# A hybrid mixer and MLP layer on one core: masked score copies on all partitions at once, a values pass with the width outermost, a last tile in two halves

## The chip, the cores and the metric

The kernel runs on one core of one Trainium2 chip. The metric is the device time of one execution in microseconds (us); lower is better. The kernel before takes 1099.75 us (median of 3 runs, 1098.73 to 1100.7).

The engines are called by what they do here: TensorE (PE) multiplies matrices, and PEld is its loading of the stationary operand; VectorE (DVE) and ScalarE (ACT) do elementwise work; GpSimd (POOL) does a little of it; SyncE (SP) issues most transfers. Each engine works through its instructions in program order.

## The reference

One decoder layer, 1024 tokens of width 1024, all in float32:

```python
h = rms_norm(x, norm_mix_g)
u = h @ w_in                                  # pool 256 | q 768 | f 768 | i 768 | g 768
y_pool = pool_mixer(u_pool, pool_w, pool_scale)
y_hgrn = hgrn2_mixer(q_raw, f_raw, i_raw, g_raw, lower_bounds, hgrn_norm_g)
x = x + concatenate([y_pool, y_hgrn]) @ w_out
h2 = rms_norm(x, norm_mlp_g)
x = x + square(relu(h2 @ w_up)) @ w_down
return rms_norm(x, final_norm_g)
```

The recurrent mixer has 6 heads of 128 channels. With `f = lb + (1-lb) sigmoid(z)`, `k = (1-lb) sigmoid(-z)`, `q = silu(q_raw)` and `v = i_raw`, a head's output at position t is the sum over s <= t of `(q_t * k_s * product of f from s+1 to t) . v_s`, then normed per head and gated by `silu(g_raw)`.

## The kernel before, in words

**Numbers in pairs.** Each matmul operand is split into a high and a low part: ScalarE copies it with rounding (L116, or L246 for x), VectorE subtracts (L117, L247). A product is three matmuls (`mm3`, L122 to L124): high by high, high by low, low by high.

**The start (L211 to L396).** TensorE runs 14 warm-up matmuls (L216). SyncE loads the transposed x in two halves of 512 tokens, each in four pieces of 512 KB (`load_xt`, tiles `xt`), and between the first ones the values weights of the first two heads in two pieces of 512 KB (`raw_v`). Then come four row tiles of x (`load_rows`, tiles `xn`, in the two one-buffer tags T and Kn), the weights of q (`raw_q`) and f (`raw_f`) of head 0, the second half of x, and four more row tiles. Behind these stand small constants and, in a two-buffer ring, the weights that follow. The row tiles only serve for the norm's scale: ScalarE squares and sums them (L255), VectorE and GpSimd make the reciprocal root (L257, L259), and TensorE transposes it (`pt_rms`) into `rms_row`.

For each half, TensorE first makes the values (`dense_V`, four token tiles of 256 columns, in the `dense` banks), with the token tile outside and the 8 width tiles of 128 inside; then q (`gated`) and f (`forget`). ScalarE copies the values out of their banks with the norm's scale (`scaled_V`, L298). A bank can be reused when that is done.

**The heads (L398 to L626).** TensorE's order is written out by hand. A head's recurrence is the generator `hgrn`, which yields how many steps of other work (the next head's projections, `beside`; a step is mostly three matmuls of 512 columns) TensorE does before it goes on (`LAGS`). A chunk of 128 tokens has two half chunks of 64. The scores within a half chunk are made by levels: the diagonal and the neighbours (`sc_near`), then pairs at distances 2, 4, 8, 16 and 32 (`sc`), each after the elementwise products of q and k with the decays (`deepen`, L519, L520) and ScalarE's gathering of the keys and queries (`kq`, L438, L439). The scores of a level lie in a PSUM bank of a ring of two. VectorE picks the valid ones with predicated copies into `scores`, a tile of 8 chunks by 128 x 128. Its two half chunks lie on 64 partitions each and at different columns, so the copies are made by stretches of 32 or 64 partitions: 4 with `dmask` (L424) and 4 with `lmask` (L428) for the nearest, then 4 per level (L452). The scores between half chunks (L462) are copied by ScalarE (L466, L467). Then the keys are transposed, the states chained, and the output is a product of `scores` with the values.

The forget gate's K is `sigmoid(-z)` from ScalarE (L328), multiplied by `om = 1-lb` on VectorE (L329); F is scaled on GpSimd (L330). `om` comes from a short chain at the start (L374 to L384) that uses both VectorE and ScalarE. F, Q and K have two buffers each.

**The MLP and the end (L628 to L1099).** Up and down projections run in blocks that share products; TensorE has no gap there. The final sums into x (L662) are followed by the norm. For the last two products VectorE, ScalarE and GpSimd work in written order: of each of the eight token tiles the left 512 columns come last. A tile's steps are add (VectorE, L662), squares and sum (ScalarE, L991), the mean (VectorE, L1004), the reciprocal root (GpSimd, L1006), then the two products with it (VectorE L1011, ScalarE L1012) and two stores. The products of a tile are written behind the next tile's add and squares.

Of the kernel before, what the change touches and what calls it, by code (L numbers as in the profile page):

```python
# [17 lines left out]
P = 128  # L18
# [42 lines left out]
def kernel(  # L61
# [110 lines left out]
    with ExitStack() as pa:  # L172
        cmix = pa.enter_context(tc.tile_pool(name="cmix", bufs=1))
        dmask = cmix.tile([P, 32], U8, name="dmask")
# [44 lines left out]
        def load_xt(h, b, tag, bufs=2):  # L219
            t = ha.tile([P, 2, HALF], F32, tag=tag, name=f"xt_{h}_{b}", bufs=bufs)  # L220
            nc.sync.dma_start(t, x_t_v[:, 2 * b:2 * b + 2, h * HALF:(h + 1) * HALF])
            return t

        def load_rows(i):
            t = ha.tile([P, D], F32, tag=("T", "Kn")[i % 2], name=f"xn_{i}", bufs=1)
            nc.sync.dma_start(t, x[0, i * P:(i + 1) * P, :])
# [8 lines left out]
        pool.memset(scores, 0.0)  # L235

# [5 lines left out]
        def split_xt(t, h, b):  # L242
            for e in range(2):
                j = 2 * b + e
                hi, lo = hT[h][0][:, j, :], hT[h][1][:, j, :]
                act.activation(hi, t[:, e, :], AF.Copy, scale=g1[:, j:j + 1])  # L246
                dve.scalar_tensor_tensor(  # L247
                    out=lo, in0=t[:, e, :], scalar=g1[:, j:j + 1], in1=hi.bitcast(F32), op0=ALU.mult, op1=ALU.subtract
                )
# [24 lines left out]

        def dense_V(pair, ws, i):

            if i == 0:
                for hd in (2 * pair, 2 * pair + 1):
                    vts[hd] = ha.tile([P, NT, P], F32, tag="V", name=f"V_{hd}", bufs=3)
# [44 lines left out]
        def forget(f, k, w, h, hd):  # L324
# [4 lines left out]
            dve.tensor_scalar(k, k, om[:, hd:hd + 1], None, op0=ALU.mult)  # L329
            pool.tensor_scalar(f, f, om[:, hd:hd + 1], lb[:, hd:hd + 1], op0=ALU.mult, op1=ALU.add)  # L330

        def head_tiles(hd):
            return [ha.tile([P, S], F32, tag=tag, name=f"{tag}_{hd}") for tag in "QFK"]
# [10 lines left out]
        xts, xns, w0 = {}, [], []  # L344
        for b, tag in enumerate("QQKK"):
            xts[0, b] = load_xt(0, b, tag)
            split_xt(xts[0, b], 0, b)
            if b < 2:
                c0 = V0
                w0.append(load_w(w_in_v[:, 4 * b:4 * b + 4, c0:c0 + 256], [4, 256], f"v0_{b}"))  # L350
        xns = [load_rows(i) for i in range(4)]
        wq = q_weights(0)
        wf = f_weights(0)
        for b, tag in enumerate("FFGS"):
            xts[1, b] = load_xt(1, b, tag, 2 if tag == "F" else 1)
            split_xt(xts[1, b], 1, b)
# [15 lines left out]
        act.copy(dmask, mraw[:, 2 * len(LEVELS), :])  # L372
# [31 lines left out]
        def hgrn(hd, q, f, k, vt):  # L404
# [17 lines left out]
            for g in range(4):  # L422
                pr = slice(g * 32, (g + 1) * 32)
                dve.copy_predicated(  # L424
                    sc[pr, :, pr], dmask[pr, None, :].to_broadcast([32, NT, 32]),
                    ps[pr, :256].rearrange("p (c x) -> p c x", x=32),
                )
                dve.copy_predicated(  # L428
                    strided(sc[pr], 1 + g * 32, [(HALF - 1, 2), (P, NT // 2), (2, 16)]),
                    lmask[pr, 0:2, :, g % 2 * 16:g % 2 * 16 + 16],  # L430
                    ps[pr, 256:384].rearrange("p (a c x) -> p a c x", a=2, x=16),
                )
            for li, m in enumerate(LEVELS[1:], 1):
# [15 lines left out]
                for g in range(2):  # L449
                    pr = slice(g * 64, (g + 1) * 64)  # L450
# [703 lines left out]
```

## Time and profile before

| | |
|---|---|
| median of 3 runs | 1099.75 us |
| the profiled execution | 1100.17 us |
| its span | 1098.4 us |
| mean granted clock of TensorE | 0.997 of full speed |
| busy: TensorE, VectorE, ScalarE, GpSimd | 1079.2, 791.8, 422.0, 81.9 us |
| bytes moved | 137.55 MB, 125 GB/s |

The span runs from the first instruction to the end of the last; the execution's own time is 1.8 us longer. A line of the profile names the source line, the engine, the operation, what is written from what (output<-inputs, buffer numbers left out), and the sizes (partitions x elements). In a timeline the first two numbers are the start and the duration in us; a bracket gives how long the engine was idle before it and what ended that. In a list by form, "busy, mean ns | idle before" follow the count. In a list of waits, an arrow points from the engine and line that waited to what it waited for. Matmuls overlap, and their ends are modelled.

### The profile page before, as it was taken

What the parts mean: (1) busy time and instruction counts of PE and PEld (TensorE: products, weight loads), DVE (VectorE), ACT (ScalarE), POOL (GpSimd) and SP (SyncE); (2) the same over time, 40 slices, a digit from 0 to 9 for tenths busy, and PEclk for the clock granted to TensorE, in tenths of its full rate; (3) what the DMA queues carried; (4) which work ended last, traced back from release to release, by engine and by line L of the source; (5) the groups of instructions that cost most, each with busy time, mean ns of one, the idle gap of its engine ahead of it and who ended that gap; (6) DMA issues with size and microseconds to landing.
All of it is one profiled execution on the core that took longest, in us unless ns stands there. A gap on an engine that the chain in (4) does not pass through costs nothing.

```text
span 1098.4 us, 14269 instructions
## 1 busy us (share of the span) xinstructions
PE 1079.2 (98%) x5728; PEld 894.1 (81%) x5728; DVE 791.8 (72%) x1068; ACT 422.0 (38%) x647; POOL 81.9 (7%) x124
## 2 busy tenths in 40 slices
PE   8989999999999999999999999999999999999996
PEld 6868797879887788888888888888888888888885
DVE  4498847784679861599768657855988968677774
ACT  6745343333343431444332233224244333333343
POOL 1001010101010101110011001101100000000001
PEclk9999999999999999999999999999999999999998
DMA  9521102110210162314445335427993354344104
GB/s 313 152 57 31 36 20 58 39 40 21 58 39 20 42 227 87 115 49 154 149 180 189 112 137 191 144 94 267 368 359 148 115 192 153 115 182 162 39 1 153
DMA packets 71362, 137.55 MB, mean 125 GB/s; under 512 B 4864, under 2 KB 44928, under 8 KB 67712
## 3 DMA queue, kind: packets, MB, share of 16 engines
q1 hardware_dynamic: 60656, 100.98, 27.1%
q0 software_dynamic: 9344, 33.56, 7.8%
q10 hardware_dynamic: 1296, 2.10, 0.5%
q8 instruction: 45, 0.74, 0.3%
q14 instruction: 21, 0.17, 0.1%
HBM read 98.87 MB, written 37.75 MB: 124 GB/s over the span
## 4 chain that ended last, share of the span: by engine, by line
PE 85%; DVE 8%; issue 2%; DMA 2%; ACT 2%; POOL 1%; SPq 0%; ACTq 0%; POOLq 0%
PE ps_dx L123 5%; PE ps_ua L124 5%; PE ps_ua L122 5%; PE ps_dx L124 5%; PE ps_dx L122 5%; PE ps_ua L123 5%; PE ps_o L122 3%; PE ps_dy L123 3%; PE ps_uc L124 3%; PE ps_uc L122 3%; PE ps_dy L124 3%; PE ps_dy L122 3%; PE ps_uc L123 3%; PE ps_o L123 3%; PE ps_o L124 3%
## 5 line engine op out<-in xcount | busy, mean ns | idle before, releaser
L116 ACT CAST wdop<-raw_wd 128x2048 fp32r<-128x2048 f32 x28 | 53.6, 1914 | 156.1 <-PE ps_dy L124 49.3
L122 PE MATMUL ps_ua<-h2op,whi_wu 128*128 128x512 f32 x256 | 99.7, 389 | 0.0
L124 PE MATMUL ps_ua<-h2op,wlo_wu 128*128 128x512 f32 x256 | 99.6, 389 | 0.0
L123 PE MATMUL ps_ua<-h2op,whi_wu 128*128 128x512 f32 x256 | 99.6, 389 | 0.0
L122 PE MATMUL ps_dx<-wdop,hop 128*128 128x512 f32 x256 | 99.6, 389 | 0.0
L123 PE MATMUL ps_dx<-wdop,hop 128*128 128x512 f32 x256 | 99.6, 389 | 0.0
L124 PE MATMUL ps_dx<-wdop,hop 128*128 128x512 f32 x256 | 99.6, 389 | 0.0
L117 DVE TENSOR_TENSOR wdop<-raw_wd,wdop 128x2048 fp32r<-128x2048 f32 x28 | 64.1, 2290 | 29.1 <-ACT wdop L116 29.1
L117 DVE TENSOR_TENSOR hop<-hraw,hop 128x2048 fp32r<-128x2048 f32 x28 | 64.0, 2284 | 2.9 <-ACT hop L116 2.9
L116 ACT CAST hop<-hraw 128x2048 fp32r<-128x2048 f32 x28 | 53.4, 1910 | 31.0 <-DMA hraw<-hid 19.5
L117 DVE TENSOR_TENSOR wlo_wu<-raw_wu,whi_wu 128x1024 fp32r<-128x1024 f32 x23 | 28.0, 1222 | 47.8 <-ACT whi_wu L116 47.8
L116 ACT CAST whi_wu<-wsum 128x1024 fp32r<-128x1024 f32 x22 | 23.2, 1054 | 93.9 <-DVE wsum L659 47.5
L662 DVE TENSOR_TENSOR x<-ps_dx,x 128x512 f32<-128x512 f32 x64 | 43.9, 688 | 20.3 <-PE ps_dx L124 20.3
L122 PE MATMUL ps_v<-whi_v,hT_hi 128*128 128x256 f32 x192 | 54.5, 285 | 2.5 <-ACT whi_v L116 1.9
L122 PEld LDWEIGHTS ps_dx<-wdop,hop 128*128 128x128 f32 x256 | 48.1, 188 | 10.0
L123 PEld LDWEIGHTS ps_ua<-h2op,whi_wu 128*128 128x128 f32 x256 | 48.1, 188 | 10.0
L124 PEld LDWEIGHTS ps_ua<-h2op,wlo_wu 128*128 128x128 f32 x256 | 48.1, 188 | 10.0
L123 PEld LDWEIGHTS ps_dx<-wdop,hop 128*128 128x128 f32 x256 | 48.1, 188 | 9.9
L124 PEld LDWEIGHTS ps_dx<-wdop,hop 128*128 128x128 f32 x256 | 48.1, 188 | 9.9
L122 PEld LDWEIGHTS ps_ua<-h2op,whi_wu 128*128 128x128 f32 x256 | 48.1, 188 | 9.8
L123 PE MATMUL ps_v<-wlo_v,hT_hi 128*128 128x256 f32 x192 | 54.3, 284 | 0.8 <-DVE wlo_v L117 0.8
L124 PE MATMUL ps_v<-whi_v,hT_lo 128*128 128x256 f32 x192 | 54.1, 284 | 0.0
(242 smaller groups left out, 2780.2 us busy)
## 6 DMA issues: line engine op xcount, KB each, us to landing
hid<-hid POOLq DMA_DIRECT2D x56, 512.0 KB, 3.2
hraw<-hid SPq DMA_DIRECT2D x28, 1024.0 KB, 5.2
raw_wu<-in_w_up_dram SPq DMA_DIRECT2D x32, 512.0 KB, 3.8
raw_wd<-in_w_down_dram SPq DMA_DIRECT2D x16, 1024.0 KB, 7.1
xt<-in_x_t_dram SPq DMA_DIRECT2D x8, 512.0 KB, 8.0
xn<-in_x_dram SPq DMA_DIRECT2D x8, 512.0 KB, 7.1
x<-x_mid SPq DMA_DIRECT2D x8, 512.0 KB, 5.8
raw_v<-in_w_in_dram SPq DMA_DIRECT2D x6, 512.0 KB, 3.8
```

The source lines that it names most:

```text
L116: act.copy(hi, src)
L117: dve.tensor_tensor(out=lo, in0=src, in1=hi.bitcast(F32), op=ALU.subtract)
L122: pe.matmul(ps, lh, rh, start=start, stop=False, skip_group_check=goes_on)
L123: pe.matmul(ps, lh, rl, start=False, stop=False, skip_group_check=goes_on)
L124: pe.matmul(ps, ll, rh, start=False, stop=stop, skip_group_check=goes_on)
L662: dve.tensor_tensor(out=out_, in0=a, in1=b, op=ALU.add)
```

## The change

There are five edits.

1. **Scores within a half chunk.** A new tile `within` holds, for all 128 partitions, 8 chunks of 64 columns: the scores of a partition's own half chunk. The predicated copies now work on all 128 partitions: two pairs for the nearest (even and odd blocks of 32 by a mask of two parts) and one per level, 9 a head instead of 28. When all levels are in, ScalarE copies `within` into the two diagonal blocks of `scores` with two copies of 64 partitions.
2. **K's scaling** by `om` moves from VectorE to ScalarE (`act.mul`).
3. **The start.** x and the first values weights come in pieces of 256 KB (one width tile of x, two width tiles of weights), split piece by piece. The first values pass has the width outermost: per width tile three matmuls for each of four token tiles, which share two banks of the `misc` ring of three. The row tiles lie in the six buffers that the mixer's outputs use later, and the q weights are asked for after two of them.
4. **Buffers.** F has one buffer, Q and K keep two; the second half of x borrows other tags.
5. **The last tile.** In the last product the last token tile is made in two halves of 256 columns, each with its own add, squares and sum.

The core of the diff:

```diff
+        within = ha.tile([P, NT, P // 2], F32, name="within", tag="within", bufs=1)
...
+        def load_xt(h, tags):
+            for j in range(KT):
+                if j % 2 == 0:
+                    t = ha.tile([P, 2, HALF], F32, tag=tags[j // 2][0], name=f"xt_{h}_{j // 2}", bufs=tags[j // 2][1])
+                nc.sync.dma_start(t[:, j % 2, :], x_t_v[:, j, h * HALF:(h + 1) * HALF])
+                split_xt(t[:, j % 2, :], h, j)
+                yield j
+        def first_V(h, ws):
+            banks = [misc_ps(f"ps_v0_{h}_{i}") for i in range(2)]
+            for j in range(KT):
+                w = ws[j // 4]
+                for i in range(4):
+                    c = i * P
+                    mm3(
+                        banks[i // 2][:, i % 2 * 256:(i % 2 + 1) * 256],
+                        (hT[h][0][:, j, c:c + P], hT[h][1][:, j, c:c + P]),
+                        (w[0][:, j % 4, :], w[1][:, j % 4, :]),
+                        j == 0 and i % 2 == 0, j == KT - 1, i % 2 == 1,
+                    )
+            return banks
...
-            t = ha.tile([P, D], F32, tag=("T", "Kn")[i % 2], name=f"xn_{i}", bufs=1)
+            t = mixp.tile([P, D], F32, tag="mix", name=f"xn_{i}")
...
-            dve.tensor_scalar(k, k, om[:, hd:hd + 1], None, op0=ALU.mult)
+            act.mul(k, k, om[:, hd:hd + 1])
...
-        xns = [load_rows(i) for i in range(4)]
+        xns = [load_rows(i) for i in range(2)]
         wq = q_weights(0)
+        xns += [load_rows(i) for i in range(2, 4)]
         wf = f_weights(0)
...
-            vps = [finish(dense_V(0, w0, i)) for i in (4 * h, 4 * h + 2)]
+            vps = first_V(h, w0)
...
-            for g in range(4):
-                pr = slice(g * 32, (g + 1) * 32)
+            for e in range(2):
                 dve.copy_predicated(
-                    sc[pr, :, pr], dmask[pr, None, :].to_broadcast([32, NT, 32]),
-                    ps[pr, :256].rearrange("p (c x) -> p c x", x=32),
+                    within[:, :, e * 32:(e + 1) * 32], dmask[:, e, None, :].to_broadcast([P, NT, 32]),
+                    ps[:, :256].rearrange("p (c x) -> p c x", x=32),
                 )
...
-                for g in range(2):
-                    pr = slice(g * 64, (g + 1) * 64)
-                    for a in range(2):
-                        dve.copy_predicated(
-                            strided(sc[pr], g * 64 + (a * HALF or m), [(P, NT // 2), (2 * m, 32 // m), (1, m)]),
-                            lmask[pr, 2 * li + a, :, :].rearrange("p j (n m) -> p j n m", m=m),
-                            ps[pr, a * P:(a + 1) * P].rearrange("p (j n m) -> p j n m", j=NT // 2, m=m),
-                        )
+                dve.copy_predicated(
+                    strided(within, m, [(S // 4 - m, 2), (P // 2, NT // 2), (2 * m, 32 // m), (1, m)]),
+                    lmask[:, 2 * li:2 * li + 2, :, :].rearrange("p a j (n m) -> p a j n m", m=m),
+                    ps[:, :256].rearrange("p (a j n m) -> p a j n m", a=2, j=NT // 2, m=m),
+                )
+            for g in range(2):
+                pr = slice(g * 64, (g + 1) * 64)
+                act.copy(sc[pr, :, pr], within[pr])
...
+                width = 256 if (g, n, e) == (*products[-1], 3) else 512
+                for c0 in range(0, 512, width):
+                    ns, cs = slice(c0, c0 + width), slice(dh * 512 + c0, dh * 512 + c0 + width)
...
+                    add(xs[i][:, cs], ps[:, ns], xs[i][:, cs])
+                    yield i, cs
```

How this moves instructions is seen in the order on each engine, at three places.

TensorE at the start, before. `ps_v0_0` and `ps_v0_2` are the banks of two pairs of token tiles, `whi` and `wlo` the parts of the values weights, `hT` the parts of x:

```order
L122 MATMUL ps_v0_0_273<-whi_v0_0_160,hT_hi0_144 128x256
L122 MATMUL ps_v0_2_322<-whi_v0_0_160,hT_hi0_144 128x256
L123 MATMUL ps_v0_0_273<-wlo_v0_0_161,hT_hi0_144 128x256
L124 MATMUL ps_v0_0_273<-whi_v0_0_160,hT_lo0_145 128x256
L122 MATMUL ps_v0_0_273<-whi_v0_0_160,hT_hi0_144 128x256
```

After, with the two banks of the first half:

```order
L122 MATMUL ps_v0_0_0_293<-whi_v0_0_159,hT_hi0_145 128x256
L123 MATMUL ps_v0_0_0_293<-wlo_v0_0_160,hT_hi0_145 128x256
L124 MATMUL ps_v0_0_0_293<-whi_v0_0_159,hT_lo0_146 128x256
...
L122 MATMUL ps_v0_0_1_294<-whi_v0_0_159,hT_hi0_145 128x256
L123 MATMUL ps_v0_0_1_294<-wlo_v0_0_160,hT_hi0_145 128x256
L124 MATMUL ps_v0_0_1_294<-whi_v0_0_159,hT_lo0_146 128x256
```

Each width tile now serves all four token tiles, twelve matmuls, before the next width tile is touched.

VectorE in the first head, from the first near copy to the last, before. `Q_268` and `K_270` are head 0's, `Q_653` is the next head's:

```order
L424 COPY_PREDICATED scores<-dmask,sc_near 32x8x32
L519 TENSOR_TENSOR Q_268<-Q_268,dec_648 128x2x128x2
L428 COPY_PREDICATED scores<-lmask,sc_near 32x2x4x16
L424 COPY_PREDICATED scores<-dmask,sc_near 32x8x32
L520 TENSOR_TENSOR K_270<-K_270,dec_648 128x2x128x2
L428 COPY_PREDICATED scores<-lmask,sc_near 32x2x4x16
L424 COPY_PREDICATED scores<-dmask,sc_near 32x8x32
L315 TENSOR_TENSOR Q_653<-ps_q_1_690,rms_row 128x512
L428 COPY_PREDICATED scores<-lmask,sc_near 32x2x4x16
L424 COPY_PREDICATED scores<-dmask,sc_near 32x8x32
L452 COPY_PREDICATED scores<-lmask,sc_2_734 64x4x16x2
L428 COPY_PREDICATED scores<-lmask,sc_near 32x2x4x16
```

After, from the multiply ahead of the first near copy to the last near copy; `Q_288` and `K_290` are head 0's:

```order
L549 TENSOR_TENSOR Q_288<-Q_288,dec_668 128x2x128x2
L454 COPY_PREDICATED within<-dmask,sc_near 128x8x32
L550 TENSOR_TENSOR K_290<-K_290,dec_668 128x2x128x2
L458 COPY_PREDICATED within<-lmask,sc_near 128x2x4x16
L549 TENSOR_TENSOR Q_288<-Q_288,dec_668 128x2x64x4
L454 COPY_PREDICATED within<-dmask,sc_near 128x8x32
L550 TENSOR_TENSOR K_290<-K_290,dec_668 128x2x64x4
L458 COPY_PREDICATED within<-lmask,sc_near 128x2x4x16
```

The near bank is read by four copies instead of eight, and the next level's multiplies (`128x2x64x4`) stand before the last of them instead of behind the second level's copies.

VectorE at the very end, before. The numbers after `x` and `rstd` tell the token tiles:

```order
L662 TENSOR_TENSOR x_6438<-ps_dx_3_7786,x_6438 128x512
L1011 SCALAR_TENSOR_TENSOR y<-x_6436,rstd_n_6_8296,gf 128x512
L1004 TENSOR_SCALAR ms_n_7_8317<-ss_7_0_8311,ss_8121 128x1
L1011 SCALAR_TENSOR_TENSOR y<-x_6438,rstd_n_7_8319,gf 128x512
```

After:

```order
L692 TENSOR_TENSOR x_6356<-ps_dx_3_7704,x_6356 128x256
L1041 SCALAR_TENSOR_TENSOR y<-x_6354,rstd_n_6_8214,gf 128x512
L1137 TENSOR_SCALAR ss_left<-ss_7_0_8229,ss_8039 128x1
L692 TENSOR_TENSOR x_6356<-ps_dx_3_7704,x_6356 128x256
L1034 TENSOR_SCALAR ms_n_7_8252<-ss_7_256_8250,ss_left 128x1
L1041 SCALAR_TENSOR_TENSOR y<-x_6356,rstd_n_7_8254,gf 128x512
```

The add of the last tile is in two halves, and the product of the tile before stands between them.

More of the change, by code (lines that the diff above doesn't have):

```diff
@@ L173 @@
         cmix = pa.enter_context(tc.tile_pool(name="cmix", bufs=1))
-        dmask = cmix.tile([P, 32], U8, name="dmask")
+        dmask = cmix.tile([P, 2, 32], U8, name="dmask")
         lmask = cmix.tile([P, len(LEVELS) * 2, NT // 2, 32], U8, name="lmask")
@@ L273, in finish, with values @@
                     return end.value
+        def values(pair):
+            for hd in (2 * pair, 2 * pair + 1):
+                vts[hd] = ha.tile([P, NT, P], F32, tag="V", name=f"V_{hd}", bufs=3)
         def dense_V(pair, ws, i):
             if i == 0:
-                for hd in (2 * pair, 2 * pair + 1):
-                    vts[hd] = ha.tile([P, NT, P], F32, tag="V", name=f"V_{hd}", bufs=3)
+                values(pair)
             ps = dense_ps(f"ps_v{pair}_{i}")
@@ L371 @@
             act.copy(lmask[:, li:li + 2], mraw[:, li:li + 2, None, :].to_broadcast([P, 2, NT // 2, 32]))
-        act.copy(dmask, mraw[:, 2 * len(LEVELS), :])
+        pool.memset(dmask, 0)
+        for g in range(4):
+            pr = slice(g * 32, (g + 1) * 32)
+            act.copy(dmask[pr, g % 2, :], mraw[pr, 2 * len(LEVELS), :])
         mx = small.tile([P, NH], F32, tag="lbt", name="lb_shift")
@@ L547, in pool_input @@
                 yield from dense_T(by_chunk(u, h), w, h, f"pool{kt}")
-            wins = [ha.tile([P, S], F32, tag=tag, name=f"win{tag}_{kt}") for tag in "KF"]
+            wins = [ha.tile([P, S], F32, tag=tag, name=f"win{tag}_{kt}", bufs=1 if tag == "F" else 2) for tag in "KF"]
             prev = u
@@ L987, with squares @@
         xs, sss = [None] * NT, [None] * NT
-        def squares(i, dh):
-            ss = small.tile([P, 1], F32, tag="ss3", name=f"ss3_{i}_{dh}", bufs=16)
-            act.activation(junk, xs[i][:, dh * 512:(dh + 1) * 512], AF.Square, accum_out=ss)
+        def squares(i, cs):
+            ss = small.tile([P, 1], F32, tag="ss3", name=f"ss3_{i}_{cs.start}", bufs=16)
+            act.activation(junk[:, :cs.stop - cs.start], xs[i][:, cs], AF.Square, accum_out=ss)
             return ss
@@ L1093 @@
             for (g, n), (pools, a, b) in zip(products[-2:], ((pools, a, b), ahead)):
-                for i in product(g, n, a, b):
-                    ss = squares(i, 0)
+                for i, cs in product(g, n, a, b):
+                    ss = squares(i, cs)
                     if ready:
                         final_rows(*ready)
-                    ready = i, row_scale(i, ss)
+                        ready = None
+                    if cs.stop == 256:
+                        both = small.tile([P, 1], F32, tag="part", name=f"ss_{i}_left", bufs=8)
+                        dve.tensor_scalar(both, ss, 1.0 / D, sss[i], op0=ALU.mult, op1=ALU.add)
+                        sss[i] = both
+                    else:
+                        ready = i, row_scale(i, ss)
             final_rows(*ready)
```

63 lines of the change are left out of this document (30 added, 33 removed).

## The prediction

> **What bounds the kernel now.** I read the page first, then the busy times by stage, then the list of what TensorE waited for, and last the timelines of the stages in which it waits.
>
> ```profile
> span 1098.4 us, 14269 instructions
> PE 1079.2 (98%) x5728; PEld 894.1 (81%) x5728; DVE 791.8 (72%) x1068; ACT 422.0 (38%) x647; POOL 81.9 (7%) x124
> ```
>
> TensorE is busy for 98% of the span. A change that takes no matmul away can win only from the other 19.2 us. The busy times by stage say where those lie:
>
> ```profile
> 0.00:60.00 60.00, 55.53 (x329) 46.99 (x330) 27.11 (x41) 43.40 (x77) 5.32 (x14) 1.00 0.70 224
> 60.00:120.00 60.00, 56.36 (x411) 44.01 (x410) 55.56 (x118) 24.32 (x51) 4.52 (x5) 1.00 0.13 36
> 400.00:1080.00 680.00, 680.00 (x3033) 563.59 (x3032) 493.96 (x485) 239.93 (x261) 45.15 (x82) 1.00 0.42 154
> 1080.00:1098.40 18.40, 9.29 (x41) 7.35 (x40) 7.16 (x14) 6.58 (x14) 2.70 (x5) 0.85 0.46 171
> ```
>
> After each stage stand its length, then PE, PEld, DVE, ACT, POOL, the granted clock, the DMA share and GB/s. From 400 to 1080 TensorE has no gap. It loses 4.5 us in the first 60, 3.6 us in the next 60 (there VectorE is busy for 55.6 of 60), and 9.1 us at the end. TensorE's waits by name (us in total, times, longest):
>
> ```profile
> PE ps_v L122 <- ACT whi_v L116: 1.9, 1, 1.9
> PE sc L444 <- DVE scores L428: 1.4, 2, 1.1
> PE sc L444 <- ACT kq L438: 1.1, 1, 1.1
> PE sc_near L402 <- DVE d L412: 1.1, 1, 1.1
> PE sc L462 <- DVE scores L452: 0.8, 1, 0.8
> PE ps_v L123 <- DVE wlo_v L117: 0.8, 1, 0.8
> PE ps_v L122 <- ACT V L298: 0.6, 1, 0.6
> PE ps_o L122 <- DVE mix L533: 0.5, 1, 0.5
> PE pto L531 <- DVE mix L573: 0.5, 1, 0.5
> PE ptk L477 <- DVE K L520: 0.2, 1, 0.2
> ```
>
> Three of them are the first values pass (1.9 + 0.8 + 0.6), five are the heads' score work (1.4 + 1.1 + 1.1 + 0.8 + 0.2), and two are the end of the mixer (0.5 + 0.5). From 400 to 1080 a matmul starts every 680 / 3033 = 0.224 us, yet the rows of such matmuls (below) last 0.39 or 0.40. A row thus reaches into the time of the next, and a wait costs TensorE up to 0.17 us more than its row says: I add 0.15 us for each.
>
> **The start.** ScalarE's, VectorE's and TensorE's timelines:
>
> ```profile
> 4.61 1.33 ACT L246 ACTIVATE hT_hi<-xt,g 128x512 fp32r<-128x512 f32 x2 [1.91 <-DMA xt<-in_x_t_dram]
> 6.52 1.04 ACT L116 CAST whi_v<-raw_v 128x1024 fp32r<-128x1024 f32 x1 [0.58 <-DMA raw_v<-in_w_in_dram]
> ...
> 10.74 2.68 ACT L246 ACTIVATE hT_hi<-xt,g 128x512 fp32r<-128x512 f32 x4 [0.30 <-DMA xt<-in_x_t_dram]
> ...
> 16.40 1.05 ACT L116 CAST whi_q<-raw_q 128x1024 fp32r<-128x1024 f32 x1 [0.56 <-DMA raw_q<-in_w_in_dram]
> ...
> 21.74 1.06 ACT L255 ACTIVATE squares<-xn 128x1024 bf16<-128x1024 f32 x1 [2.50 <-DMA xn<-in_x_dram]
> ```
>
> ```profile
> 5.36 1.42 DVE L247 SCALAR_TENSOR_TENSOR hT_lo<-xt,g,hT_hi 128x512 fp32r<-128x512 f32 x2 [4.24 <-ACT hT_hi L246]
> 7.60 1.22 DVE L117 TENSOR_TENSOR wlo_v<-raw_v,whi_v 128x1024 fp32r<-128x1024 f32 x1 [0.82 <-ACT whi_v L116]
> ...
> 17.48 1.23 DVE L117 TENSOR_TENSOR wlo_q<-raw_q,whi_q 128x1024 fp32r<-128x1024 f32 x1 [3.13 <-ACT whi_q L116]
> ```
>
> ```profile
> 20.66 0.40 PE L122 MATMUL ps_q<-hT_hi,whi_q 128*128 128x512 f32 x1
> ...
> 32.86 0.39 PE L122 MATMUL ps_v<-whi_v,hT_hi 128*128 128x256 f32 x1 [0.64 <-ACT V L298]
> ...
> 44.47 0.40 PE L122 MATMUL ps_q<-hT_hi,whi_q 128*128 128x512 f32 x1
> ```
>
> Each of the first transfers ends a wait of ScalarE. Between the second (6.52) and the fifth (10.74) lie three of 512 KB, 1.41 us each, so a 256 KB piece at that rate takes 0.70. The first piece lands between 4.61 and 0.70 before it, since all that precedes it is the same; I take the middle, 4.25, and the weight piece 0.70 later, 4.95. ScalarE's first half takes 1.33 / 2 = 0.67 (to 4.92), its weight half 1.04 / 2 = 0.52 (to 5.47). TensorE's warm-up ends at 5.7, so the first matmul is no longer kept waiting. The second needs VectorE's low part: 4.92 + 0.71 + 0.61 = 6.25. It stood at 7.60 + 1.22 = 8.82 before. The second half's pass, without a gap, is 96 matmuls from 32.86 to 44.47, 0.121 each; 95 from 6.3 end at 17.8, against 20.66. Gain 2.9 us.
>
> The pass must then be fed. Two steps of the width bring three pieces, 2.1 us of transfer; ScalarE works 2 x 0.67 + 0.52 = 1.9 on them, VectorE 2 x 0.71 + 0.61 = 2.0, TensorE 24 x 0.121 = 2.9. TensorE stays the slowest, so width outermost costs nothing once it has started.
>
> What comes next does not move as far. The weights of q have the same bytes queued ahead of them, so they land at 16.4 as now, and their low part ends at 17.48 + 1.23 = 18.7. The third matmul of q needs it; with the pass over at 17.8 and two matmuls of 0.23 done, TensorE waits 0.5 us that it did not wait before.
>
> The row loads stop waiting for each other's buffers, which SyncE's list shows:
>
> ```profile
> SPq L226 <- ACT squares L255: 9.6, 5, 5.7
> ```
>
> Behind them in SyncE's order are the weights of f and the second half of x. The fourth row tile can now follow the q weights by two transfers of 1.4, at 19.2 instead of 21.7, and with it the scales and the copies out of the first pass's banks come about 2.5 us sooner, in step with TensorE. Of the wait of 0.6 + 0.15 for those banks I let 0.2 stand, since the copies of the second bank come behind the whole second half of x on ScalarE. The start wins 2.9 - 0.5 + 0.55 = 3.0 us.
>
> **The score copies.** Costs by form, and VectorE's timeline in the first head:
>
> ```profile
> L452 DVE COPY_PREDICATED scores<-lmask,sc 64x128 f32<-64x128 uint8 x120 | 33.9, 325 | 1.6
> L424 DVE COPY_PREDICATED scores<-dmask,sc_near 32x256 f32<-32x256 uint8 x24 | 10.6, 442 | 0.7 <-PE sc_near L402 0.3
> L328 ACT ACTIVATE K<-K 128x512 f32<-128x512 f32 x12 | 7.6, 632 | 0.3
> L466 ACT COPY scores<-sc 64x256 f32<-64x256 f32 x6 | 2.1, 354 | 9.4 <-PE sc L462 9.4
> ```
>
> ```profile
> 65.84 0.69 DVE L519 TENSOR_TENSOR Q<-Q,F 128x512 f32<-128x512 f32 x1
> 66.44 0.69 DVE L520 TENSOR_TENSOR K<-K,F 128x512 f32<-128x512 f32 x1
> ...
> 67.64 0.42 DVE L424 COPY_PREDICATED scores<-dmask,sc_near 32x256 f32<-32x256 uint8 x1
> ...
> 73.26 0.44 DVE L428 COPY_PREDICATED scores<-lmask,sc_near 32x128 f32<-32x128 uint8 x1
> ```
>
> A head's 28 copies (4 of L424, 4 of L428, 20 of L452) cost about 8 x 0.44 + 20 x 0.325 = 10.0 us and become 9. The near ones keep their elements per partition, so 0.44. A level's copy has 256 elements per partition on 128 partitions, a form not shown: from below 0.33 (the half as long one), from above 0.88 (twice the near one); I take 0.44, the row of equal length. Nine at 0.44 are 4.0 us, so VectorE is rid of 6 us a head, and of K's two scalings, which go to ScalarE.
>
> On the path: the near bank was freed at 73.26 + 0.44 = 73.7, 6.1 us after the first copy started, and TensorE's level at distance 4, the next user of that bank, waited 1.1 us for it. Now four near copies and four half-width multiplies (0.60 from start to start) stand in that stretch: 4.2 us, so it is freed 1.9 sooner and both waits on L428 go (1.4 + 2 x 0.15 = 1.7). The multiplies for the level at distance 8 now stand ahead of that point, so the wait on kq goes (1.25). The wait on L452 goes with the shorter queue (0.95), the one on K with the scaling's move (0.3). The wait for d shrinks: K's scaling stood ahead of it on VectorE, and the weights that ScalarE waits for are asked for sooner; of 1.1 + 0.15 I take 0.9. Together 5.1 us.
>
> ScalarE pays per head 2 x 0.63 for K and two copies of 64x512, from 0.35 (the half as long row) to 0.7. That is 2.5 us a head on an engine that is idle for 36 of the 60 us of the second stage, and nobody waits for it at once. K's scaling in the first head lies beside GpSimd's scaling of F; without that cover it would cost 0.63 once. Before K's first scaling ScalarE now also waits for the lower bounds; next q's weights, behind it, are needed only when f is done, so this costs nothing. The new memsets lie in the idle start of GpSimd, and F with one buffer is read out before the next head writes it: nothing.
>
> The two waits at the mixer's end stay: VectorE has no score copies left there.
>
> **The last tile.** VectorE, then ScalarE:
>
> ```profile
> 1089.33 0.69 DVE L662 TENSOR_TENSOR x<-ps_dx,x 128x512 f32<-128x512 f32 x1 [1.02 <-PE ps_dx L124]
> ...
> 1091.68 0.75 DVE L1011 SCALAR_TENSOR_TENSOR y<-x,rstd_n,gf 128x512 f32<-128x512 f32 x1 [0.66 <-POOL rstd_n L1006]
> ```
>
> ```profile
> 1090.05 0.63 ACT L991 ACTIVATE junk<-x 128x512 bf16<-128x512 f32 x1 [1.38 <-DVE x L662]
> ```
>
> Half-width add and squares save at most 0.34 + 0.31. Twice as many matmuls at 0.121 for 0.224 cost 24 x 0.121 - 12 x 0.224 = 0.2. In VectorE's order the last product of the tile before (0.75) now stands between the two adds and waits for that tile's scale, and ScalarE's scaling of it stands before the last squares. Between a gain of 0.5 and a loss of 0.3 I take a gain of 0.1.
>
> **The sum.** 3.0 + 5.1 + 0.1 = 8.2 us off the profiled 1100.17 us (span 1098.4 and what lies around it) is 1092.0. The median of the runs is 0.4 lower, so I forecast 1091.6 us. About 0.2%, 2.2 us, can be told from no change.
>
> **The rivals.** *The start gives its gain back.* The pass ends sooner but q, f and the second half each wait for their own transfers; TensorE reaches f's end as now. For it: ScalarE's rows that end on DMA; against it: row loads no longer hold SyncE. 8.2 - 3.0 leaves 5.2: 1094.6 us. Chance 0.12.
>
> *The wide copies are dear.* At 0.88 or more each, four of them and four multiplies take 5.9 us, the bank is freed as late as now, and the waits on L428, L452 and half of kq stay: 3.3 us less won, 1094.9 us. Chance 0.12.
>
> *Small pieces (slower).* If a piece cost what one costs alone, 2.0 us (the lone 256 KB stores at the end), the twelfth would land 4.25 + 11 x 2.0 = 26 instead of 12:
>
> ```profile
> DMA to landing us min/median/max: 2.0/2.0/2.6
> ```
>
> Everything behind would come 14 us later: 1091.6 + 14 = 1105.6 us. It decides from pieces 1.45 us apart (0.70 + 8.2 / 11). Against it: three transfers landed 1.41 apart with others in flight, though each is longer than that from issue to landing. Chance 0.04. The Trainium skill, "DMA: Bandwidth & Descriptors", sections "Anatomy of one DMA" and "Bandwidth", speaks for this rival: it gives each transfer about 2.0 us fixed plus its bytes at 436 GB/s, and wants 1 MiB and more to a transfer. By that fit, an estimate, a lone piece is 2.6 us, and twelve in a row would make it 1112 us; the trace of queued loads disagrees, since 512 KB each came every 1.41 us where the fit gives 3.2.
>
> *Nothing.* Both gains fail together, and no more than 2 us is left: 1098.5 us, chance 0.04. My forecast keeps 0.68.
>
> The range reaches down to 1089 (no new wait for q, the mixer's end and a 4.0 us first landing won as well) and up past the first two rivals to 1096. Faster 0.92, same 0.04, slower 0.04.
>
> **What would show it.** Right: TensorE's second values matmul at about 6.3, q's first at about 17.8 with a short wait after it, no wait of TensorE on score copies, nine copies a head near 0.44 us. Wrong: pieces more than 1 us apart, level copies near 0.9, TensorE waiting on ScalarE's K or on the copies from within to scores.

## The result, and the profile after

The changed kernel takes 1092.88 us (median of 4 runs, 1092.24 to 1093.55), the kernel before 1099.89 us beside it. The ratio is 0.9937, with a 95% interval of 0.992 to 0.9954. The change makes the kernel faster, by about 7 us. The profiled execution took 1093.07 us, with a span of 1091.3 us against 1098.4, so the span lost 7.1 us.

The head of the page after, then the busy times of three stages (columns as before):

```profile
span 1091.3 us, 14220 instructions
PE 1078.6 (99%) x5740; PEld 895.3 (82%) x5740; DVE 753.8 (69%) x946; ACT 438.7 (40%) x678; POOL 81.9 (8%) x126
```

```profile
0.00:60.00 60.00, 57.75 (x336) 48.61 (x337) 28.66 (x45) 45.88 (x84) 6.34 (x16) 1.00 0.69 230
60.00:120.00 60.00, 60.00 (x447) 47.03 (x448) 48.47 (x92) 29.28 (x58) 4.18 (x4) 1.00 0.13 39
1073.00:1091.30 18.30, 8.97 (x50) 7.57 (x48) 7.30 (x15) 6.37 (x15) 2.28 (x5) 0.89 0.46 171
```

TensorE's gap in the second stage (3.6 us) is closed, and VectorE works 48.5 of its 60 us instead of 55.6. In the first stage TensorE still loses 2.3 us, where it lost 4.5. The last stage is as poor as it was. TensorE's waits after:

```profile
...
PE ps_dx L122 <- DVE x L692: 0.7, 1, 0.7
PE ps_o L122 <- DVE mix L563: 0.6, 1, 0.6
PE ps_f L124 <- DVE wlo_f L117: 0.5, 1, 0.5
PE ps_q L124 <- DVE wlo_q L117: 0.5, 1, 0.5
PE pto L561 <- DVE mix L603: 0.5, 1, 0.5
```

No wait on score copies, on `kq`, on K or on `d` is left. The two at the mixer's end stand as before. Three are new: `wlo_q`, which was forecast, and `wlo_f` and the last tile's bank (`ps_dx`, on VectorE's add), which were not. (The line left out is the warm-up's, ahead of all useful work.)

Where the time came from is read from TensorE's timeline, since TensorE has hardly a gap from 400 us to the last tile in either kernel: the start of the same matmul in both says how far ahead the changed kernel is. The rows of before that the prediction does not show, then those of after:

```profile
64.12 0.42 PE L402 MATMUL sc_near<-d,ones 128*32 128x256 f32 x4
...
69.14 0.34 PE L444 MATMUL sc<-kq 128*64 128x64 f32 x4
...
91.52 0.44 PE L477 MATMUL ptk<-ident,K 128*128 128x128 f32 x2
...
384.40 0.50 PE L122 MATMUL ps_o<-whi_wo,mT_hi 128*128 128x512 f32 x1
```

```profile
17.85 0.50 PE L122 MATMUL ps_q<-hT_hi,whi_q 128*128 128x512 f32 x1
...
31.26 0.28 PE L122 MATMUL ps_v<-whi_v,hT_hi 128*128 128x256 f32 x1
...
62.42 0.42 PE L433 MATMUL sc_near<-d,ones 128*32 128x256 f32 x4
...
66.23 0.39 PE L474 MATMUL sc<-kq 128*64 128x64 f32 x5
...
86.14 0.38 PE L507 MATMUL ptk<-ident,K 128*128 128x128 f32 x2
...
376.67 0.47 PE L122 MATMUL ps_o<-whi_wo,mT_hi 128*128 128x512 f32 x1
```

| the same matmul | before | after | ahead by | won since the row above |
|---|---|---|---|---|
| q's first (first half) | 20.66 | 17.85 | 2.8 | 2.8 |
| second values pass | 32.86 | 31.26 | 1.6 | -1.2 |
| head 0, `sc_near` | 64.12 | 62.42 | 1.7 | 0.1 |
| head 0, first level | 69.14 | 66.23 | 2.9 | 1.2 (the wait for `d`) |
| head 0, keys turned | 91.52 | 86.14 | 5.4 | 2.5 |
| mixer's end, `ps_o` | 384.40 | 376.67 | 7.7 | 2.3 |
| end of the span | 1098.4 | 1091.3 | 7.1 | -0.6 |

In this pair of profiles the start thus won 1.7 us, the score work 6.0, and the end lost 0.6. Three terms of the sum were off, and they partly cancel. The experiments ask why. Single rows of the start move by up to 1 us from one execution to the next, as the profiles below show, so the second row of the table (-1.2) is not to be read alone.

### The profile page after: what moved, and what is told of

Its sections match the earlier page's. It is cut to its first block, busy times and chain, and to the rows that moved or that the text cites. A ratio compares the mean times of both kernels' runs of the same rounds, so it can differ in the third digit from the quotient of the medians.

```text
span 1091.3 us, 14220 instructions
## 1 busy us (share of the span) xinstructions
PE 1078.6 (99%) x5740; PEld 895.3 (82%) x5740; DVE 753.8 (69%) x946; ACT 438.7 (40%) x678; POOL 81.9 (8%) x126
## 4 chain that ended last, share of the span: by engine, by line
PE 94%; DVE 2%; DMA 1%; issue 1%; SPq 0%; POOL 0%; ACT 0%; POOLq 0%; ACTq 0%
PE ps_ua L124 5%; PE ps_ua L122 5%; PE ps_ua L123 5%; PE ps_dx L123 5%; PE ps_dx L124 5%; PE ps_dx L122 5%; PE ps_o L122 3%; PE ps_dy L123 3%; PE ps_uc L122 3%; PE ps_uc L124 3%; PE ps_dy L124 3%; PE ps_dy L122 3%; PE ps_uc L123 3%; PE ps_o L124 3%; PE ps_o L123 3%; PE ps_f L122 2%
## 5 line engine op out<-in xcount | busy, mean ns | idle before, releaser
L122 PE MATMUL ps_dx<-wdop,hop 128*128 128x512 f32 (+1 forms) x260 | 100.4, 386 | 0.7 <-DVE x L692 0.7
L123 PE MATMUL ps_dx<-wdop,hop 128*128 128x512 f32 (+1 forms) x260 | 100.3, 386 | 0.0
L124 PE MATMUL ps_dx<-wdop,hop 128*128 128x512 f32 (+1 forms) x260 | 100.3, 386 | 0.0
L692 DVE TENSOR_TENSOR x<-ps_dx,x 128x512 f32<-128x512 f32 (+1 forms) x65 | 43.9, 677 | 19.9 <-PE ps_dx L124 19.9
```

The source lines that it names most:

```text
L122: pe.matmul(ps, lh, rh, start=start, stop=False, skip_group_check=goes_on)
L123: pe.matmul(ps, lh, rl, start=False, stop=False, skip_group_check=goes_on)
L124: pe.matmul(ps, ll, rh, start=False, stop=stop, skip_group_check=goes_on)
L692: dve.tensor_tensor(out=out_, in0=a, in1=b, op=ALU.add)
```

## The experiments

Every ratio is against the kernel before, run on the same chip beside the experiment, with its 95% interval.

### Each part alone

**The wide copies** (edit 1, with the buffers that make room for them):

```diff
-                for g in range(2):
-                    pr = slice(g * 64, (g + 1) * 64)
-                    for a in range(2):
-                        dve.copy_predicated(
...
+                dve.copy_predicated(
+                    strided(within, m, [(S // 4 - m, 2), (P // 2, NT // 2), (2 * m, 32 // m), (1, m)]),
...
+                act.copy(sc[pr, :, pr], within[pr])
```

> The kernel before with the wide score copies alone (and the buffers that make room for them); K's scaling stays on VectorE, start and tail stay. Theory 1 (VectorE's long queue of narrow copies held TensorE in every head): nearly all of the 6.0 us that the score work won in the changed kernel comes from here, 4.5 to 5.7 us faster than before, about 1094.8 us, and the waits on lines L428 and L452 of the kernel before are gone. Theory 2 (the heads won because the start shifted the weights' transfers, the copies only follow): under 2 us faster. By the prediction's terms (1.7 + 1.25 + 0.95 + most of 0.9): 4.5 us.

Measured: 1094.94 us, ratio 0.9956 (0.9944 to 0.9968), 4.9 us faster. The waits on score copies, `kq` and K are gone; of the wait for `d` (1.1) there remains this row:

```profile
PE sc_near L407 <- DVE d L417: 0.4, 1, 0.4
```

Theory 1 holds: the copies alone win most of what the score work won. The time may understate it: in this profile TensorE's granted clock was 0.50 from 10 to 12 us (1.00 in the kernel before), and q's first matmul came at 21.80, 1.1 us later than before, although the start is the old one. Between the same two matmuls, from the first `sc_near` to `ps_o`, it takes 314.9 us; the kernel before takes 320.3 and the changed kernel 314.25, so the copies win 5.4 of the 6.0.

**The start** (edits 3 and 4):

```diff
-            t = ha.tile([P, D], F32, tag=("T", "Kn")[i % 2], name=f"xn_{i}", bufs=1)
+            t = mixp.tile([P, D], F32, tag="mix", name=f"xn_{i}")
...
-            vps = [finish(dense_V(0, w0, i)) for i in (4 * h, 4 * h + 2)]
+            vps = first_V(h, w0)
```

> The kernel before with the start alone (256 KB pieces, width outermost, row tiles in the mixer's buffers, and the borrowed buffers). Theory 1 (the first pass wins 2.8 us, and the waits for the low parts of q and f and the late second half give 1.1 us back): 1.5 to 2.0 us faster than before, about 1098.0 us, with a new wait of 0.5 us on wlo_q and one of 0.5 us on wlo_f. Theory 2 (the prediction's 3.0 us, of which the heads eat a part because VectorE starts them from further behind): TensorE is 3.0 us ahead at the end of f of the second half, and under that later.

Measured: 1096.45 us, ratio 0.9965 (0.9952 to 0.9977), 3.4 us faster: more than either theory said. The wait on `wlo_q` came (0.5), that on `wlo_f` did not. The heads do not eat the start's gain, they add to it. The wait for `d` is gone, though all narrow copies are still there, as its list shows:

```profile
PE sc L470 <- DVE scores L454: 0.9, 2, 0.5
PE sc L488 <- DVE scores L478: 0.9, 1, 0.9
```

**The last tile in halves** (edit 5), and **K's scaling on ScalarE** (edit 2):

```diff
+                width = 256 if (g, n, e) == (*products[-1], 3) else 512
...
+                for c0 in range(0, 512, width):
```

```diff
-            dve.tensor_scalar(k, k, om[:, hd:hd + 1], None, op0=ALU.mult)
+            act.mul(k, k, om[:, hd:hd + 1])
```

> The kernel before with the last tile in two halves alone. Theory 1 (the right half's first matmul waits for VectorE's add of the left half, because both lie in one bank, and twice as many matmuls cost 0.2 us): 0.4 to 0.8 us slower than before, about 1100.4 us. Theory 2 (the prediction's: half-width add and squares outweigh the matmuls): 0.1 us faster; the loss of the tail seen in the changed kernel would then belong to something else, such as the order of its stores.

> The kernel before with K's scaling on ScalarE alone. Theory 1 (it takes 1.2 us a head from VectorE's queue, where about 6 us stand in the way): 0.3 to 1.2 us faster than before. Theory 2 (ScalarE's 0.72 us form, behind its gathering of keys and queries, delays K by as much as VectorE wins): between 0.3 us faster and 0.5 us slower.

Measured: the halves 1100.62 us, ratio 1.0008 (0.9999 to 1.0016), 0.8 us slower; K's scaling 1099.15 us, ratio 0.9994 (0.9986 to 1.0002), 0.7 us faster. Each interval touches no change, so the times alone do not settle either. K's scaling shortens the wait for `d` (0.7 instead of 1.1) and takes away that for `kq` (1.1), but TensorE then waits longer for K at the key transposes (1.1 instead of 0.2) and for the copies of L428 (1.7 instead of 1.4).

Added up, the four parts make 4.9 + 3.4 - 0.8 + 0.7 = 8.2 us, 1.2 more than the change. The intervals of the four times are too wide to tell that from nothing (each reaches 0.9 to 1.4 us either way), but the profiles show one cause, the wait for `d`, won more than once: from `sc_near` to the first level TensorE takes 5.02 us in the kernel before, 1.25 less with the start alone, 0.66 less with the copies alone, 0.33 less with K's scaling alone, 2.2 together, but only 1.2 less with all.

### What in the start wins

The start's 3.4 us were split by two kernels: the row tiles alone (in the mixer's six buffers, with q's weights after two of them), and the rest alone (256 KB pieces, width outermost).

```diff
-            t = ha.tile([P, D], F32, tag=("T", "Kn")[i % 2], name=f"xn_{i}", bufs=1)
+            t = mixp.tile([P, D], F32, tag="mix", name=f"xn_{i}")
...
-        xns = [load_rows(i) for i in range(4)]
+        xns = [load_rows(i) for i in range(2)]
         wq = q_weights(0)
+        xns += [load_rows(i) for i in range(2, 4)]
```

> The kernel before with one part of the start: the row tiles in the mixer's six buffers and q's weights after two of them; pieces of 512 KB and the token tile outermost as before. Theory 1 (SyncE's wait for the row tiles' buffers was what held the second half, the masks and the next weights back): the first pass ends at about 20.6 us as before, but TensorE's waits for the first banks (0.6 us) and for d (1.1 us) shrink or go, and 1.5 to 2.6 us are won, about 1097.6 us. Theory 2 (the early first pass carries the start's 3.4 us): under 0.8 us.

> The kernel before with the rest of the start: 256 KB pieces and the width outermost, with the row tiles in their two one-buffer tags and q's weights after all four. Theory 1: the first pass ends 2.5 us sooner, but q, f and the second half come when their transfers let them, so 0.3 to 1.2 us are won, about 1099.0 us, and the wait for d stays. Theory 2: 2.4 to 3.4 us are won, about 1097.0 us.

Measured: the rows alone 1097.43 us, ratio 0.9975 (0.9965 to 0.9986), 2.55 us faster; the pass alone 1099.19 us, ratio 0.999 (0.9982 to 0.9999), 0.8 us faster. Together that is the start's 3.4. Theory 1 holds in both: what looks like the main part, the early first pass, is the smaller one. With it alone TensorE comes to the heads sooner than `d` does, and waits for it longer than before (1.1):

```profile
PE sc_near L427 <- DVE d L437: 1.8, 1, 1.8
```

It is the buffers that win, and not the order: SyncE asks for q's weights behind two row tiles in the kernel before as well (at 8.85 us there, at 8.77 with the rows alone). How they win is a chain of queues. SyncE's and ScalarE's timelines, before:

```profile
35.82 1.37 SPq L226 DMA_DIRECT2D xn<-in_x_dram  x2
...
43.01 0.33 SPq L361 DMA_DIRECT2D mraw<-in_masks_dram  x1
...
49.98 0.38 SPq L158 DMA_DIRECT2D raw_g<-in_w_in_dram  x1
```

```profile
41.84 1.06 ACT L255 ACTIVATE squares<-xn 128x1024 bf16<-128x1024 f32 x1 [1.26 <-DMA xn<-in_x_dram]
...
45.68 1.94 ACT L371 CAST lmask<-mraw 128x256 uint8<-128x256 int32 x6 [0.21 <-DMA mraw<-in_masks_dram]
...
54.01 1.05 ACT L116 CAST whi_g<-raw_g 128x1024 fp32r<-128x1024 f32 x1 [3.36 <-DMA raw_g<-in_w_in_dram]
54.97 0.58 ACT L265 COPY rms_row<-pt_rms 128x512 f32<-128x512 f32 x1
```

and with the row tiles alone moved:

```profile
23.10 0.33 SPq L362 DMA_DIRECT2D mraw<-in_masks_dram  x1
...
44.59 0.37 SPq L158 DMA_DIRECT2D raw_g<-in_w_in_dram  x1
```

```profile
36.26 1.04 ACT L255 ACTIVATE squares<-xn 128x1024 bf16<-128x1024 f32 x1
...
49.89 0.58 ACT L265 COPY rms_row<-pt_rms 128x512 f32<-128x512 f32 x1
```

The last two row tiles waited on SyncE for a buffer until 35.82, so ScalarE squared the last of them at 41.84. The masks take one of the same two buffers (tag Kn) and were asked for at 43.01, when these squares were done. Behind the squares ScalarE works in order: the copies of the values, the masks, the rounding of q's next weights. When VectorE has split those, a raw buffer comes free, and `raw_g` was asked for at 49.98; ScalarE's copy of the second half's scales stood behind the wait for it. Each link comes 5 to 6 us sooner once the tiles have buffers of their own. The masks come 20 us sooner, but ScalarE had waited only 0.21 us for them: it is the last squares that held it. VectorE's products of the second half follow, and `d` behind them.

**Pieces of 512 KB with the width outermost**, in the changed kernel:

```diff
-                nc.sync.dma_start(t[:, j % 2, :], x_t_v[:, j, h * HALF:(h + 1) * HALF])
+                    nc.sync.dma_start(t, x_t_v[:, j:j + 2, h * HALF:(h + 1) * HALF])
...
-                nc.sync.dma_start(raw[:, ks], w_in_v[:, j:j + 2, V0:V0 + 256])
+                nc.sync.dma_start(raw, w_in_v[:, 4 * b:4 * b + 4, V0:V0 + 256])
```

> The changed kernel with pieces of 512 KB as before, and the width still outermost. Theory 1 (the width outermost lets the pass begin early, the smaller pieces are worth only the first landing): the pass starts about 1.4 us later and waits for pieces, but q and f then wait less for their weights (up to 1.0 us in all), so it is 0.3 to 1.0 us slower than the changed kernel, about 1093.6 us. Theory 2 (the size of the pieces carries the start's gain): 1.7 us or more slower, 1094.6 us or more. Theory 3 (small pieces cost transfer time, and later transfers gain by large ones): faster than the changed kernel.

Measured: 1093.37 us, ratio 0.9948 (0.9934 to 0.9961), 0.5 us above the changed kernel's first median and 0.9 above its second (below). At q's first matmul it is 2.0 us later than the changed kernel's start is on average (four profiles, here and below: 17.85 to 18.64), at the second values pass 0.9 later (30.30 to 31.26). Theory 1 holds: about half of an early first pass is handed back within the same half, for TensorE no longer waits on `wlo_q`. ScalarE rounds q's weights at 16.09 here, and at 16.75 to 17.32 in those four.

### The order of the loads, and a landing that varies

The changed kernel with the weights of q and f asked for ahead of the row tiles:

```diff
+        wq = q_weights(0)
         xns = [load_rows(i) for i in range(2)]
-        wq = q_weights(0)
-        xns += [load_rows(i) for i in range(2, 4)]
         wf = f_weights(0)
+        xns += [load_rows(i) for i in range(2, 4)]
```

> The changed kernel with q's weights asked for ahead of the first two row tiles, and f's ahead of the last two. Theory 1 (the order of the transfers holds q and f back): q's weights land about 2.7 us sooner and f's about 2 us sooner, the waits of 0.5 us on wlo_q and on wlo_f go, and the whole is 0.8 to 1.2 us faster than the changed kernel, about 1091.9 us; the scales come 1.5 us later, which nobody waits for yet. Theory 2 (the row tiles' scales are next in line, so the gain goes into a wait for the values' banks or for q's banks): within 0.3 us of the changed kernel.

Measured: 1092.04 us, ratio 0.9932 (0.9919 to 0.9944), 0.8 us under the changed kernel's first median, 0.4 under its second. Both waits on low parts are gone, and a wait for the row scales, which theory 2 named, has taken the place of one:

```profile
24.99 0.66 PE L286 MATMUL pt_rms<-ident,rb 128*128 128x128 f32 x4 [0.61 <-DVE rb L283]
```

With the last tile whole again as well, and beside it the changed kernel once more:

> The changed kernel with q's and f's weights asked for ahead of the row tiles and the last tile whole. Theory 1 (two separate places): 0.85 us of the order and 0.9 us of the tile add up, about 1091.1 us. Theory 2 (the order of the loads only moves the landing within what varies from run to run): 1091.7 us, as with the whole tile alone.

> The changed kernel itself, beside the kernel with both places mended. Theory 1 (in its profiled execution the fourth row tile's squares started at 20.93 us, in the same start of the kernel with the interleaved last tile at 19.90): the landing of that tile varies by about 1 us, TensorE's second values pass starts between 30.3 and 31.3 us with it, and the time lies at 1092.2 to 1093.2 us. Theory 2 (the landing is fixed and the mended tail moved the schedule): the second pass starts at 31.26 us again.

Measured: 1091.62 us, ratio 0.9918 (0.9905 to 0.9932), and for the changed kernel 1092.45 us, ratio 0.9927 (0.9914 to 0.9941). Mending both places gives the lowest median of this study, but 0.8 us under the changed kernel and not 1.7, and the intervals overlap. By time its theory 2 fits: the whole tile alone, with the loads in the old order, takes 1091.71 us (below), so by the medians the order adds 0.1 us to it, though the second values pass starts at 30.26 and 30.09 us in the two kernels with the new order, ahead of every other. What the order is worth stays open. What varies from run to run is seen at the fourth row tile. ScalarE's squares of it in the changed kernel's first profile, its second, and the kernel with the interleaved tail (below), all with the same start:

```profile
20.93 1.06 ACT L277 ACTIVATE squares<-xn 128x1024 bf16<-128x1024 f32 x1 [1.73 <-DMA xn<-in_x_dram]
```

```profile
20.31 1.06 ACT L277 ACTIVATE squares<-xn 128x1024 bf16<-128x1024 f32 x1 [0.55 <-DMA xn<-in_x_dram]
```

```profile
19.90 1.06 ACT L277 ACTIVATE squares<-xn 128x1024 bf16<-128x1024 f32 x1 [0.57 <-DMA xn<-in_x_dram]
```

The second values pass starts at 31.26, 30.72 and 30.30, so it looks as if TensorE followed the tile's landing one for one. It does so only in the first profile. There the tile comes 4.2 us behind q's weights on ScalarE, and TensorE waits on `wlo_f`, behind the scales, the copies of V and `whi_f` on ScalarE; from q's first matmul to the second values pass it takes 13.4 us. In the four other profiles with this start (the second one, the interleaved tail, the whole tile and the start alone) the tile comes 2.9 to 3.1 us behind, TensorE does not wait on `wlo_f`, and it takes 12.0 to 12.3 us. The wait on `wlo_f` was thus that execution's bad luck, worth about 1.1 us.

What the other four differ by lies further ahead. The 14 warm-up matmuls last 4.8 to 6.1 us in the five profiles. Before, the first pass waited for weights anyway and hid this; now it starts right behind the warm-up (5.6 to 6.8 us), in two of the profiles it then waits 0.3 us for a low part of x, and q's first matmul comes at 17.85 to 18.91. The second profile's time and its second pass lie where theory 1 put them, but not by its mechanism. A shorter warm-up was not tried.

### The last tile

In the changed kernel, the last tile whole again:

```diff
-                width = 256 if (g, n, e) == (*products[-1], 3) else 512
```

> The changed kernel with its last tile whole again, as before. Theory 1 (the halves cost 0.7 us for the wait on the bank that both share, and 0.2 us of matmuls, less what they save): 0.6 to 0.8 us faster than the changed kernel, about 1092.2 us. Theory 2 (the loss of 0.8 us with the tail alone lies within the spread of the runs): no difference, 1092.9 us.

And still in halves, but with the whole tile before it between them:

```diff
+            if (g, n) == products[-1]:
+                steps[2:] = (3, 0, 256), (2, 0, 512), (3, 256, 256)
```

> The changed kernel with the last product's order changed: left half of the last tile, then the whole tile before it, then the right half, so that VectorE's add of the left half lies beside matmuls of another bank. Theory 1 (it is the wait on the shared bank that makes the halves lose): TensorE's wait of 0.7 us goes, and the end is 0.7 to 1.0 us sooner than in the changed kernel, about 1092.0 us, or a little under the whole tile. Theory 2 (the loss lies behind the matmuls, in the order of VectorE's and ScalarE's last steps): within 0.3 us of the changed kernel, though the wait is gone.

Measured: whole, 1091.71 us, ratio 0.9928 (0.9916 to 0.994); between, 1092.15 us, ratio 0.993 (0.9918 to 0.9942). VectorE's rows, from the add of the third-last tile to the last product. The changed kernel:

```profile
1076.17 0.69 DVE L692 TENSOR_TENSOR x<-ps_dx,x 128x512 f32<-128x512 f32 x1 [1.02 <-PE ps_dx L124]
...
1084.58 0.75 DVE L1041 SCALAR_TENSOR_TENSOR y<-x,rstd_n,gf 128x512 f32<-128x512 f32 x1 [0.66 <-POOL rstd_n L1036]
```

the whole tile:

```profile
1075.58 0.69 DVE L692 TENSOR_TENSOR x<-ps_dx,x 128x512 f32<-128x512 f32 x1 [1.02 <-PE ps_dx L124]
...
1083.37 0.75 DVE L1041 SCALAR_TENSOR_TENSOR y<-x,rstd_n,gf 128x512 f32<-128x512 f32 x1 [0.66 <-POOL rstd_n L1036]
```

and the tile between:

```profile
1075.22 0.69 DVE L692 TENSOR_TENSOR x<-ps_dx,x 128x512 f32<-128x512 f32 x1 [1.02 <-PE ps_dx L124]
...
1081.01 0.41 DVE L692 TENSOR_TENSOR x<-ps_dx,x 128x256 f32<-128x256 f32 x1
1081.75 0.75 DVE L1041 SCALAR_TENSOR_TENSOR y<-x,rstd_n,gf 128x512 f32<-128x512 f32 x1 [0.32 <-POOL rstd_n L1036]
1082.41 0.21 DVE L1034 TENSOR_SCALAR ms_n<-ss,ss_left 128x1 f32<-128x1 f32 x1
1083.28 0.75 DVE L1041 SCALAR_TENSOR_TENSOR y<-x,rstd_n,gf 128x512 f32<-128x512 f32 x1 [0.66 <-POOL rstd_n L1036]
```

From add to last product it is 8.41 us in halves, 7.79 whole and 8.06 between. So the halves cost 0.6 us, and the wait on the shared bank is a cause: without it 0.35 comes back. Split at the start of TensorE's last matmul, the three are 6.22 + 2.19, 5.02 + 2.77 and 5.29 + 2.77. Without the wait TensorE's part is 0.9 shorter, but the 0.6 that the halves save behind the matmuls is gone: there the product of the tile before (1081.75) stands ahead of the last mean (1082.41) on VectorE, as theory 2 said. In time, only the sign of the halves' cost repeats: 0.8 slower alone, 0.7 to 1.2 faster when taken out, 0.4 faster when taken out beside the new order of the loads.

## Why the prediction was right, and where it was not

The mechanism was right and the time near (1091.6 forecast, 1092.88 measured). That it was so near is partly luck, since the errors have both signs: by the profile the start won 1.3 us less than forecast and the end 0.7 less, the score work 0.9 more. By its own steps:

- *"The start wins 2.9 - 0.5 + 0.55 = 3.0 us."* It won 1.7 in the profile, and 1.6 on average: the second values pass starts at 32.16 to 32.86 us in three profiles with the old start (the kernel before, the halves alone, K's scaling alone) and at 30.30 to 31.26 in five with the new. q's first matmul came at 17.85, forecast 17.8, but at 18.00 to 18.91 in the other four: the first pass starts behind the warm-up, at 5.60 to 6.77 us instead of 5.7, and in two of them it then waits 0.3 us for a low part of x. The new wait on `wlo_q` came (0.5). The step that failed is *"they land at 16.4 as now"*, and with it the fourth row tile *"at 19.2"*. Only two raw buffers serve the weights, so q's are asked for when VectorE has split the first half of the values weights: at 8.71 to 8.85 us with the old start, 9.05 to 9.98 with the new. They land 7.5 to 7.8 us after that in both, and ScalarE rounds them at 16.75 to 17.81. The fourth row tile follows by 2.9 to 3.1 us in four profiles, near the 2.8 forecast; in the first it came about 1.1 us later still, and a wait on `wlo_f` was added. The 0.55 for the first banks was read from one execution: that wait is 0.6 us in the kernel before, 0.3 with the halves alone, and none with K's scaling alone, all with the same start.
- *"The wait for d shrinks ... of 1.1 + 0.15 I take 0.9"*, put down to the copies. All of it goes (1.2), and the row tiles' buffers alone do it. The prediction had read SyncE's 9.6 us of waiting for these buffers, but followed it only to the first half's banks, and not to the masks, the next weights and the scales behind them in the queues.
- *The score copies, 5.1.* They won 6.0. Without `d` that is 4.2 forecast and 4.8 measured. The waits went as forecast, and if nothing else was won there, each cost about 0.25 us more than its row says (4.8 us for rows of 3.5 in all, five waits), where 0.15 was assumed. The price of the wide copies was nearly right (0.50 us a level for 0.44, 0.45 a near one), as costs by form show:

```profile
L479 DVE COPY_PREDICATED within<-lmask,sc 128x256 f32<-128x256 uint8 x30 | 14.9, 498 | 19.7 <-PE sc L474 19.7
L354 ACT ACTIVATE K<-K,om 128x512 f32<-128x512 f32 x12 | 8.7, 724 | 1.2 <-DVE om L414 0.9
L486 ACT COPY scores<-within 64x512 f32<-64x512 f32 x12 | 7.4, 618 | 28.9 <-DVE within L479 28.8
...
L454 DVE COPY_PREDICATED within<-dmask,sc_near 128x256 f32<-128x256 uint8 x12 | 5.3, 445 | 0.7 <-PE sc_near L433 0.7
```

- *The last tile, a gain of 0.1.* It lost 0.6. Its saving was right: from the last matmul's start to the last product's it is 2.19 us instead of 2.78, 0.59 less (0.65 forecast). The step that failed is the matmuls' price, *"24 x 0.121 - 12 x 0.224 = 0.2"*: it takes the right half to follow at once. TensorE's rows:

```profile
1080.00 0.28 PE L124 MATMUL ps_dx<-wdop,hop 128*128 128x256 f32 x1
1080.97 0.38 PE L122 MATMUL ps_dx<-wdop,hop 128*128 128x256 f32 x1 [0.69 <-DVE x L692]
```

  The right half's first matmul comes 0.97 us after the left half's last, not 0.12: it waits until VectorE has read the left half out of the bank that both share. The Trainium skill, "PSUM — Partial Sum Buffer", section "PSUM bank collisions raise a hardware error", says that two engines must not touch one bank in the same partitions at the same time, whatever the addresses, and that semaphores should guard PSUM by bank and group of 32 partitions, or more simply by bank, but not by address; by that rule this wait was to be expected, and the trace agrees with its 0.69 us.
- *The rivals.* "The start gives its gain back" is half true of the first profile, where 1.2 of the 2.8 us were handed back before the second pass; over the four others it is 0.3 of 2.1. "The wide copies are dear" is not: 0.50 us a level. "Small pieces" is not: the third of the twelve (x's second) ends a wait of ScalarE at 6.24 us, and the twelfth (x's last) is split at 12.34, so nine pieces took at most 6.1 us, 0.68 each, where the rival needed 1.45. Only the first pieces were slow: from x's first (split at 3.69) to its second, two pieces took 2.55 us or more. A fixed 2.0 us thus does not add up over the transfers of SyncE's queue. The Trainium skill, "DMA: Bandwidth & Descriptors", section "Anatomy of one DMA", gives its 2.0 us for one transfer on GpSimd's path, which none of these took; the prediction had left that condition out.

```profile
6.24 1.38 ACT L243 ACTIVATE hT_hi<-xt,g 128x512 fp32r<-128x512 f32 x2 [1.32 <-DMA xt<-in_x_t_dram]
...
12.34 0.72 ACT L243 ACTIVATE hT_hi<-xt,g 128x512 fp32r<-128x512 f32 x1
```

- *"ScalarE ... costs nothing."* True of the time as far as seen, but K's scaling now waits 0.9 us for `om` (row L354). With that wait, the scaling itself (0.72) and the mask's four small copies (0.90 for 0.21), the rounding of `raw_g` goes to 51.37 us, from 49.03 with the start alone. The second `d` then ends at 62.88 us, as TensorE's sums over the first do (62.42 + 0.42): that cover is used up.

What stays open: how much of the 0.8 us between the changed kernel and the mended one is real, since the intervals overlap; why the warm-up lasts longer in some executions; and halves in two banks, or with VectorE's last steps in another order, which were not tried.

## What to carry to other kernels

Follow a queue that waits for a buffer through everything that stands behind it, on the next engines too: here six free buffers for eight small tiles were worth 2.55 us, three times the early first pass that they came with. Gains of parts do not add when two of them remove the same wait, so give each wait one owner. Read the start from several profiles before pricing its waits. Before a last tile is split, see that its halves lie in different PSUM banks, and that nothing of the tile before stands between the last add and the last store; that this pays was not run here.

## What the runs showed of the hardware

A predicated copy of 256 elements takes 0.44 us on 128 partitions as on 32; only the first level, whose runs are 2 elements long, takes 0.73 (that the runs are the reason is not shown). A matmul that waited costs more than its row: the third of f (wait 0.53) starts 0.93 us after the second, not 0.23, so it cost 0.70. And one row tile, behind the same queue, was used 4.2 us behind the weights ahead of it in one execution, and 2.9 to 3.1 in four others. VectorE, in the first head:

```profile
68.94 0.73 DVE L479 COPY_PREDICATED within<-lmask,sc 128x256 f32<-128x256 uint8 x1
...
71.90 0.44 DVE L479 COPY_PREDICATED within<-lmask,sc 128x256 f32<-128x256 uint8 x1
```

```profile
25.20 0.40 PE L123 MATMUL ps_f<-hT_lo,whi_f 128*128 128x512 f32 x1
26.13 0.50 PE L124 MATMUL ps_f<-hT_hi,wlo_f 128*128 128x512 f32 x1 [0.53 <-DVE wlo_f L117]
```
